# Thirty-one expert blocks in a new order, a block's transposes inside the next block's products, the first gather in one piece

## The chip, the cores and the metric

The program runs on one core of a Trainium2 chip. The metric is the device time of one execution in microseconds (us). One execution was also taken by the hardware profiler, and all rows below come from it.

## What is computed

Two transformer blocks follow each other on 256 tokens of width 1024, in float32. The change lies in the mixture of experts (MoE) at the end of the first one: 64 experts, each token goes to 8 of them, and the results are added up by token.

```python
def moe_ffn(h, router_w, router_bias, w_gate, w_up, w_down, sh_gate, sh_up, sh_down):
    ...
    scores = jax.nn.sigmoid((hf @ router_w).astype(jnp.float32))
    ...
    _, e_idx = lax.top_k(jnp.where(expert_mask, biased, -jnp.inf), TOP_K)
    gate = jnp.take_along_axis(scores, e_idx, axis=1)
    gate = gate / jnp.sum(gate, axis=-1, keepdims=True) * ROUTED_SCALE
    ...
    def expert_block(args):
        xb, e = args
        return (jax.nn.silu(xb @ w_gate[e]) * (xb @ w_up[e])) @ w_down[e]
    yb = lax.map(expert_block, (xin, block_expert)).reshape(n_rows, d)
    routed = jax.ops.segment_sum(yb * row_gate[:, None], row_tok, num_segments=T + 1)[:T]
    shared = (jax.nn.silu(hf @ sh_gate) * (hf @ sh_up)) @ sh_down
    return (routed + shared).reshape(b, s, d)
```

Each of an expert's three matrices (w_gate, w_up, w_down; 1024 x 256 or 256 x 1024 float32) is 1 MiB, so all experts together are 192 MiB.

## The kernel before

**Blocks.** Once the router's result is known, the experts are ranked by their number of tokens; the two experts 0 and 1 are fixed at ranks 0 and 1, so that their weights can be loaded ahead. `CAPS` gives each rank a capacity in slots: ranks 0 and 1 have 128, ranks 2 and 3 have 256, ranks 4 to 11 have 128, the next 20 have 64, the last 32 have 32. A block is 128 slots: one expert of 128, half of one of 256, two experts of 64 or four of 32. That makes 32 blocks. `PH` holds a phase for each kind, and the blocks of each kind are spread evenly by it; the order is, by number of experts in a block, 1 1 4 1 1 2 4 1 1 2 4 1 2 1 4 2 1 2 4 1 2 4 1 2 4 1 2 1 4 2 1 2 (the pairs "1 1" with one weight set are the halves of ranks 2 and 3).

**A block's work on TensorE**, which runs in the order of the program text (as SyncE does; the other engines' order is set by a scheduler after the start of the stage):

- every fourth block `onehots` (VectorE, tile `D`) compares slots with token positions, `gather` (L1400, tile `xgp`, evacuated to `xg` by ScalarE) fetches the tokens of four blocks by 32 products of 512 columns, and `slots` (L1384, tile `sp`) makes the scatter matrices;
- `gate_up(b)` (L1442, tile `gu`): eight products for w_gate and eight for w_up of each expert. Blocks of two or four experts put their experts side by side into 64 or 32 columns of the array (`tile_position`); each float32 product is two TensorE instructions, so a block of one expert shows as x32, of two as x64, of four as x128;
- ScalarE's Silu and one VectorE operation make `act`;
- `down(b)`: two transposes of `act` (L1459, tile `at`), ScalarE's copy to `aT` (L1461), products with w_down (L1468, tile `dn`), then `y` in two float32r parts by VectorE, ScalarE and GpSimd (L1476 to L1478; VectorE in place of GpSimd in the last two blocks);
- `scatter(b)` (L1490, tile `sc`) for two blocks at a time, 16 products of 512 columns added to the tokens.

The loop calls `gate_up(b + 1)`, then, for every second b, `scatter` of the two finished blocks, then `down(b)`.

**Weights.** `Stream` lists the loads in the order in which the blocks need them; SyncE issues one as soon as a buffer of 1 MiB is free (14 of them: 5 `wraw`, 6 `mraw`, 3 of `whi` and `wlo` together), and goes by a list in strict order. Which experts are to be loaded is known only when the router is done (`eid`).

**The start of the stage.** `shared_up(m)` (L1078, tile `sh`) issues m of the 32 products of the shared expert to fill TensorE while VectorE works out the routing. The first gather takes only the first block's 128 columns; the other 384 follow after the first block's products.

Of the kernel before, what the change touches and what calls it, by code (L numbers as in the profile page):

```python
# [18 lines left out]
F32 = mybir.dt.float32  # L19
# [7 lines left out]
T = 256  # L27
ALPHA = 2.0 ** 0.25
TOPG = 4
SHARED = int('16')  # L30
PH = {1: 0.7, 2: 0.95, 4: 0.1}
FIXED = int('2')
CAPS = ((128, FIXED), (256, 2), (128, 10 - FIXED), (64, 20), (32, 32))


class Stream:
# [86 lines left out]
def build(ctx, tc, I, out, dbg=None, stop=None):  # L123
# [640 lines left out]
    for i in range(4):  # L764
        p = plin("pyb")
# [317 lines left out]
    blocks = []  # L1083
    r0 = 0
    for c, n in CAPS:
        r = r0
        while r < r0 + n:
            if c >= 128:
                for q in range(c // 128):
                    blocks.append([(r, 128 * q, 128)])  # L1090
                r += 1
            else:
                blocks.append([(r + m, 0, c) for m in range(128 // c)])
                r += 128 // c
        r0 += n
    NBL = len(blocks)

    kinds = {}
    for b in blocks[FIXED:]:
        k = kinds.setdefault(len(b), [])  # L1100
        if b[0][1]:
            k[-1].append(b)
        else:
            k.append([b])
    place = [((i + PH[n]) / len(k), u) for n, k in kinds.items() for i, u in enumerate(k)]
    blocks = blocks[:FIXED] + [b for _, u in sorted(place, key=lambda q: q[0]) for b in u]
    def onehots(gi, Dt, lo=0, hi=4):

        bl = blocks[4 * gi:4 * gi + hi]
# [59 lines left out]
    neg_exp(1, pr1)  # L1169
    A.activation(x2h[:, 1, :], xnm[:, 1, :], AF.Copy)  # L1170
    psh += [pacc("sh0"), plin("sh1")]
    shared_up(16)
    scores(1)

    gsc = rtemp("gsc", (128, 2, 8))
# [116 lines left out]
    io256 = moe.tile([128, 256], F32, name="io256")  # L1292
    G.iota(io256, pattern=[[1, 256]], base=1, channel_multiplier=0, allow_small_or_imprecise_dtypes=True)
    D0 = moe.tile([128, 2, 512], F32R, tag="D", name="D0", bufs=1)
    onehots(0, D0, 0, 1)
    low(1)
    gsum = rtemp("gsum", (128, 2, 1))
    V.tensor_reduce(gsum, gt_, axis=AX.X, op=OP.add)
    V.reciprocal(gsum, gsum)
    for t in range(2):  # L1300
        V.tensor_scalar(gt_[:, t, :], gt_[:, t, :], gsum[:, t, :], 2.5, op0=OP.mult, op1=OP.mult)
    onehots(0, D0, 1, 4)
    dump("sel", sel.bitcast(F32), lambda d: d.rearrange("(t p) e -> p t e", p=128))
    dump("gate", gt_, lambda d: d.rearrange("(t p) e -> p t e", p=128))

# [70 lines left out]
    def slots(gi, Dt):  # L1376

        bl = blocks[4 * gi:4 * gi + 4]
        St = moe.tile([128, 4, 256], F32R, tag="S", name=f"S{gi}", bufs=2)
        gc = moe.tile([128, 4], F32, tag="gc", name=f"gc{gi}", bufs=2)  # L1380
        for b in range(4):
            p = paux(f"sp{gi}_{b}")
            for t in range(2):
                PE.matmul(p[:, 128 * t:128 * t + 256], Dt[:, t, 128 * b:128 * b + 128], idg[:, t, :],  # L1384
                          start=(t == 0), stop=(t == 1), skip_group_check=True)
            A.activation(St[:, b, :].rearrange("p (t n) -> p t n", t=2),
                         p[:, :384].rearrange("p (t n) -> p t n", t=3)[:, 0::2, :], AF.Copy)
            for k, (r, _, c) in enumerate(bl[b]):
                s_ = slice(c * k, c * k + c)
                V.tensor_scalar(gc[s_, b:b + 1], p[s_, 128 + r:129 + r], p[s_, 192 + r:193 + r], None, op0=OP.add)  # L1390
        return St, gc
# [23 lines left out]
    def pairs(b):  # L1415
        return [list(enumerate(blocks[b]))]

    def gate_up(b):
        gi, bb = divmod(b, 4)
        if bb == 0:  # L1420
            if gi:
                Dt = moe.tile([128, 2, 512], F32R, tag="D", name=f"D{gi}", bufs=1)
                onehots(gi, Dt)
            else:
                Dt = D0
            xg = tail.tile([128, 8, 512], F32, tag="big2", name=f"xg{gi}")
            grp[gi] = [None, None, xg, Dt]
            if gi:
                gather(gi, Dt, xg)
                grp[gi][:2] = slots(gi, Dt)  # L1430
            else:
                gather(gi, Dt, xg, 0, 128)
                gate_slots()
                shared_end()
        xg = grp[gi][2]
        p = plin(f"gu{b}")
        for ex in pairs(b):
            for w, off in (("g", 0), ("u", 256)):
                wts = [wtile(r, w) for _, (r, _, _) in ex]
                for j in range(8):  # L1440
                    for (k, (r, b0, c)), wt in zip(ex, wts):
                        PE.matmul(p[c * k:c * k + c, off:off + 256], xg[:, j, 128 * bb + c * k:128 * bb + c * k + c],  # L1442
                                  wt[j], start=(j == 0), stop=(j == 7), tile_position=(0, c * k))
                for _, (r, _, _) in ex:
                    wdone(r, w)
        if b == 0:
            grp[gi][:2] = slots(gi, grp[gi][3])
            gather(gi, grp[gi][3], xg, 128, 512)
        act = moe.tile([128, 256], F32, tag="act", name=f"act{b}", bufs=2)
        A.activation(act, p[:, 0:256], AF.Silu)  # L1450
        last_act[0] = V.scalar_tensor_tensor(act, act, grp[gi][1][:, bb:bb + 1], p[:, 256:512], op0=OP.mult, op1=OP.mult)  # L1451
        return act

    last_sub = [None]

    def down(b, act):
        p = paux(f"at{b}")
        for j in range(2):
            PE.transpose(p[:, 128 * j:128 * j + 128], act[:, j::2], ident)  # L1459
        aT = moe.tile([128, 2, 128], F32, tag="aT", name=f"aT{b}", bufs=2)  # L1460
        A.activation(aT, p[:, :256].rearrange("p (j s) -> p j s", j=2), AF.Copy)  # L1461
        pd = [paux(f"dn{b}_{h}") for h in range(2)]
        for ex in pairs(b):
            wts = [wtile(r, "d") for _, (r, _, _) in ex]
# [9 lines left out]
        for h in range(2):  # L1474
            hs_ = slice(512 * h, 512 * h + 512)
            V.tensor_mul(yf[:, h, :], pd[h], g2[:, hs_])  # L1476
            A.activation(y[:, 0, hs_], yf[:, h, :], AF.Copy)  # L1477
            last_sub[0] = (V if b >= NBL - 2 else G).tensor_sub(y[:, 1, hs_], yf[:, h, :], y[:, 0, hs_].bitcast(F32))  # L1478
        return y

    def scatter(b, ys):

        St, bb = grp[b // 4][0], b % 4
        for t in range(2):
            for h in range(2):
                p = plin(f"sc{b}_{t}{h}")
                q = 0
                for m in range(2):
                    for k in range(2):
                        PE.matmul(p, St[:, bb + m, 128 * t:128 * t + 128], ys[m][:, k, 512 * h:512 * h + 512],  # L1490
                                  start=(q == 0), stop=(q == 3))
                        q += 1
                o = acc[:, t, 512 * h:512 * h + 512]
                if b == NBL - 2:
                    V.scalar_tensor_tensor(o, p, 1.0, o, op0=OP.mult, op1=OP.add, accum_out=sums[:, 0, t, h:h + 1])
                elif b == 0:
                    V.scalar_tensor_tensor(o, o, ALPHA, p, op0=OP.mult, op1=OP.add)
                else:
                    V.tensor_add(o, o, p)
# [42 lines left out]
    overflow()  # L1542
    ws.ahead = 1
    for b in range(NBL):
        nxt = gate_up(b + 1) if b + 1 < NBL else None
        if len(ys) == 2:
            scatter(b - 2, ys)
            ys = []
        ys.append(down(b, act))
        act = nxt  # L1550
        if b == 2:
            prepare_loads()
# [5 lines left out]
    ln2 = ws.take_raw(ln2_req)  # L1558
    ln2g, ln2b = ln2[:, 0:D], ln2[:, D:2 * D]
    rg = moe.tile([128, 2, D], F32, tag="mraw", name="rg", bufs=6)  # L1560
    scatter(NBL - 2, ys)

    flag = nc.values_load(ovi[0:1, 0:1], min_val=0, max_val=64 * T)
    with tc.If(flag > 0):
# [413 lines left out]
```

## Time and profile before

| | |
|---|---|
| median of 3 runs | 1369.22 us (1369.01 to 1376.6) |
| the profiled execution | 1372.89 us, its span 1371.1 us |
| the MoE stage, first expert product to end of the last scatter | 511.6 to 1022.4 us of the span |
| TensorE (PE) busy | 1284.9 us, 94% of the span |
| VectorE, ScalarE, GpSimd busy | 60%, 41%, 13% |
| HBM read | 377.59 MB |

A span's time is counted from its own start. The profile's page cuts the span into 40 slices of 34.3 us; counted from 0, slices 15 to 29 hold the MoE stage.

### The profile page before, as it was taken

The numbers are of one execution on the slowest core, as the hardware profiler recorded it, in microseconds if no ns is written. First come the engines' busy times: TensorE is split into PE (matmuls) and PEld (weight loads), VectorE is DVE, ScalarE is ACT, GpSimd is POOL, SyncE is SP. The second block draws the span as 40 slices with busy tenths as digits, with TensorE's granted clock in tenths as the row PEclk, the third lists the DMA queues.
The fourth block names the chain that finished last, engine by engine and source line by source line (L and its number), as shares of the span: only waits on it lengthen the run. The fifth ranks groups of instructions, "written<-read, shape, count | busy, mean of one in ns | idle before, by whom it ended". The sixth has DMA issues, their size and how long they took to land.

```text
span 1371.1 us, 22687 instructions
## 1 busy us (share of the span) xinstructions
PE 1284.9 (94%) x9042; PEld 1051.5 (77%) x9042; DVE 818.2 (60%) x1331; ACT 567.7 (41%) x862; POOL 178.3 (13%) x169
## 2 busy tenths in 40 slices
PE   3989999999999899999999999999988999899997
PEld 1989988789899687757675756667648887899985
DVE  2999998978898731222223232221255577788995
ACT  1675644445654422313131313223126655666642
POOL 1011243411100100221111111211110000000000
PEclk9999999999999979999999999999998999999999
DMA  9967776669788476989899999999995334455550
GB/s 340 324 220 261 247 237 224 214 217 314 239 306 285 173 298 257 383 308 368 337 419 401 417 411 419 418 418 418 418 335 174 128 118 154 137 182 183 176 184 32
DMA packets 148977, 380.21 MB, mean 277 GB/s; under 512 B 7839, under 2 KB 97285, under 8 KB 129028
## 3 DMA queue, kind: packets, MB, share of 16 engines
q1 hardware_dynamic: 145856, 373.20, 74.3%
q0 software_dynamic: 2240, 5.34, 1.3%
q8 instruction: 72, 1.18, 0.3%
q10 hardware_dynamic: 772, 0.19, 0.1%
q14 instruction: 37, 0.30, 0.1%
HBM read 377.59 MB, written 1.10 MB: 276 GB/s over the span
## 4 chain that ended last, share of the span: by engine, by line
PE 61%; DVE 4%; issue 3%; ACT 2%; DMA 1%; POOL 0%; POOLq 0%; DVEq 0%; ACTq 0%
PE gu L1442 16%; PE dn L1468 8%; PE xgp L1400 5%; PE sc L1490 4%; PE pgt L555 2%; PE pgt L556 2%; PE pgt L557 2%; PE pvl L557 2%; PE pvl L555 2%; PE pvl L556 2%; PE pf L907 1%; PE pf L909 1%; PE pf L905 1%; DVE wlo L199 1%; PE sh L1078 1%
## 5 line engine op out<-in xcount | busy, mean ns | idle before, releaser
L195 ACT ACTIVATE whi<-wraw 128x1024 fp32r<-128x1024 f32 x216 | 228.1, 1058 | 240.9 <-PE pf L909 30.8
L199 DVE TENSOR_TENSOR wlo<-wraw,whi 128x1024 fp32r<-128x1024 f32 x216 | 271.1, 1257 | 64.2 <-ACT whi L195 62.9
L1442 PE MATMUL gu<-mraw,xg 128*32 128x256 f32 (+2 forms) x944 | 147.0, 380 | 0.3 <-DMA mraw<-in_w_up_dram 0.3
L1478 POOL TENSOR_TENSOR y<-yf,y 128x512 fp32r<-128x512 f32 x60 | 76.8, 1280 | 441.3 <-ACT y L1477 441.3
L1451 DVE SCALAR_TENSOR_TENSOR act<-act,gc,gu 128x256 f32<-128x256 f32 x32 | 15.4, 480 | 190.3 <-ACT act L1450 190.2
L1442 PEld LDWEIGHTS gu<-mraw,xg 128*32 128x32 f32 (+2 forms) x944 | 96.5, 136 | 29.9 <-issue 7.8
L1476 DVE TENSOR_TENSOR yf<-dn,g 128x512 f32<-128x512 f32 x64 | 44.2, 691 | 93.3 <-PE dn L1468 93.3
L1450 ACT ACTIVATE act<-gu 128x256 f32<-128x256 f32 x32 | 12.3, 384 | 199.2 <-PE gu L1442 199.2
L1442 PE MATMUL gu<-wraw,xg 128*32 128x256 f32 (+2 forms) x672 | 93.6, 380 | 0.0
L1477 ACT ACTIVATE y<-yf 128x512 fp32r<-128x512 f32 x64 | 40.3, 630 | 123.4 <-DVE yf L1476 123.4
L557 PE MATMUL pl<-hh,wlo 128*128 128x256 f32 x256 | 74.4, 292 | 4.2 <-DVE wlo L199 4.2
L1442 PEld LDWEIGHTS gu<-wraw,xg 128*32 128x32 f32 (+2 forms) x672 | 58.3, 130 | 23.9 <-DVE yf L1476 2.5
L1468 PE MATMUL dn<-wraw,aT 128*32 128x512 f32 (+2 forms) x232 | 69.5, 598 | 6.9 <-ACT aT L1461 6.9
L1468 PE MATMUL dn<-mraw,aT 128*32 128x512 f32 (+2 forms) x208 | 69.4, 598 | 6.2 <-ACT aT L1461 6.2
L555 PE MATMUL pl<-hh,whi 128*128 128x256 f32 x256 | 73.9, 289 | 0.0
L556 PE MATMUL pl<-hl,whi 128*128 128x256 f32 x256 | 73.7, 288 | 0.0
L431 DVE SCALAR_TENSOR_TENSOR adac<-wraw,csil,adac 128x1024 f32<-128x1024 f32 x49 | 67.1, 1370 | 5.9 <-DMA wraw<-in_w_ada_dram 5.3
L1490 PE MATMUL sc<-y,S 128*128 128x512 f32 x256 | 65.2, 405 | 0.1
L1400 PE MATMUL xgp<-D,x2h 128*128 128x512 f32 (+2 forms) x144 | 61.1, 424 | 0.9 <-DVE D L1118 0.9
L1402 ACT ACTIVATE xg<-xgp,mvp 128x512 f32<-128x512 f32 (+2 forms) x72 | 52.5, 730 | 19.1 <-PE xgp L1400 14.6
L1400 PE MATMUL xgp<-D,x2l 128*128 128x512 f32 (+2 forms) x144 | 58.8, 408 | 0.3 <-DVE x2l L1070 0.3
L1490 PEld LDWEIGHTS sc<-y,S 128*128 128x128 f32 x256 | 47.3, 188 | 14.9 <-issue 3.1
(575 smaller groups left out, 3565.2 us busy)
## 6 DMA issues: line engine op xcount, KB each, us to landing
wraw<-in_w_in_dram SPq DMA_DIRECT2D x56, 1024.0 KB, 6.2
wraw<-in_w_ada_dram SPq DMA_DIRECT2D x47, 1024.0 KB, 7.2
wraw<-in_w_up_dram SPq DMA_DIRECT2D x39, 1024.0 KB, 9.5
wraw<-in_w_down_dram SPq DMA_DIRECT2D x38, 1024.0 KB, 4.9
mraw<-in_w_up_dram SPq DMA_DIRECT2D x30, 1024.0 KB, 13.0
mraw<-in_w_gate_dram SPq DMA_DIRECT2D x27, 1024.0 KB, 16.1
mraw<-in_w_down_dram SPq DMA_DIRECT2D x26, 1024.0 KB, 14.9
wraw<-in_w_gate_dram SPq DMA_DIRECT2D x25, 1024.0 KB, 12.5
```

Of the source, the lines that this page charges most:

```text
L195: A.activation(hi, v, AF.Copy)
L199: V.tensor_sub(lo, v, hi.bitcast(F32))
L431: V.scalar_tensor_tensor(acc, wv[:, k, s_], c, acc, op0=OP.mult, op1=OP.add)
L555: PE.matmul(o, wh[:, k, :], xh[:, k0 + k, :], start=(k == 0), stop=False)
L556: PE.matmul(o, wh[:, k, :], xl[:, k0 + k, :], start=False, stop=False)
L557: PE.matmul(o, wl[:, k, :], xh[:, k0 + k, :], start=False, stop=(k == 7))
L1400: PE.matmul(p[:, :c1 - c0], src[:, t, j::8], Dt[:, t, c0:c1], start=(q == 0), stop=(q == 3))
L1402: A.activation(xg[:, j, c0:c1], p[:, :c1 - c0], AF.Identity, scale=mvp[:, 1, j:j + 1], bias=mvp[:, 0, j:j + 1])
L1442: PE.matmul(p[c * k:c * k + c, off:off + 256], xg[:, j, 128 * bb + c * k:128 * bb + c * k + c], wt[j], start=(j == 0), stop=(j == 7), tile ...
L1468: last_dn[0] = PE.matmul(pd[h][c * k:c * k + c, :], aT[:, j, c * k:c * k + c], wt[j][:, 512 * h:512 * h + 512], start=(j == 0), stop=(j == ...
L1478: last_sub[0] = (V if b >= NBL - 2 else G).tensor_sub(y[:, 1, hs_], yf[:, h, :], y[:, 0, hs_].bitcast(F32))
L1490: PE.matmul(p, St[:, bb + m, 128 * t:128 * t + 128], ys[m][:, k, 512 * h:512 * h + 512], start=(q == 0), stop=(q == 3))
```

## The change

The two experts at ranks 2 and 3 get 192 slots instead of 256: two blocks of 128, and a third in which the last 64 slots of both share the array. That makes 31 blocks. The order of all but the first two is written out in a table, `ORDER` (`w` stands for these three blocks in a row): 1 1 4 2 1 2 2 4 1 2 2 2 1 4 1 1 2 4 1 2 1 1 4 4 1 1 2 4 2 2 4. `down` is split: its transposes and the copy become `turn(b)`, which is called inside `gate_up(b + 1)`, between the w_gate and the w_up products. The first gather takes all 512 columns at once. `shared_up` issues 10 products instead of 16 before the routing's counts. The shared expert's last product moves from block 16 to block 8. With an odd number of blocks the last scatter holds one block (`LAST`), and VectorE makes `y`'s second part only for that one.

```diff
-SHARED = int('16')
-PH = {1: 0.7, 2: 0.95, 4: 0.1}
+SHARED = int('8')
 FIXED = int('2')
-CAPS = ((128, FIXED), (256, 2), (128, 10 - FIXED), (64, 20), (32, 32))
+CAPS = ((128, FIXED), (192, 2), (128, 10 - FIXED), (64, 20), (32, 32))
...
-            if c >= 128:
-                for q in range(c // 128):
-                    blocks.append([(r, 128 * q, 128)])
+            if c == 192:
+                blocks += [[(r, 0, 128)], [(r + 1, 0, 128)], [(r, 128, 64), (r + 1, 128, 64)]]
+                r += 2
+            elif c == 128:
+                blocks.append([(r, 0, 128)])
                 r += 1
...
+    LAST = (NBL - 1) // 2 * 2
+    aTs = {}
...
+    ORDER = "4212241222141124121144w4224"
...
-    shared_up(16)
+    shared_up(10)
...
-    onehots(0, D0, 0, 1)
+    onehots(0, D0)
     low(1)
...
-    onehots(0, D0, 1, 4)
...
-    def gate_up(b):
+    def gate_up(b, between=None):
...
-                gather(gi, Dt, xg, 0, 128)
+                gather(gi, Dt, xg)
                 gate_slots()
                 shared_end()
...
+                if w == "g" and between:
+                    between()
         if b == 0:
             grp[gi][:2] = slots(gi, grp[gi][3])
-            gather(gi, grp[gi][3], xg, 128, 512)
...
-    def down(b, act):
+    def turn(b, act):
         p = paux(f"at{b}")
         for j in range(2):
             PE.transpose(p[:, 128 * j:128 * j + 128], act[:, j::2], ident)
         aT = moe.tile([128, 2, 128], F32, tag="aT", name=f"aT{b}", bufs=2)
         A.activation(aT, p[:, :256].rearrange("p (j s) -> p j s", j=2), AF.Copy)
+        aTs[b] = aT
+
+    def down(b):
+        aT = aTs.pop(b)
...
-            last_sub[0] = (V if b >= NBL - 2 else G).tensor_sub(y[:, 1, hs_], yf[:, h, :], y[:, 0, hs_].bitcast(F32))
+            last_sub[0] = (V if b >= LAST else G).tensor_sub(y[:, 1, hs_], yf[:, h, :], y[:, 0, hs_].bitcast(F32))
...
     for b in range(NBL):
-        nxt = gate_up(b + 1) if b + 1 < NBL else None
+        if b + 1 < NBL:
+            nxt = gate_up(b + 1, lambda: turn(b, act))
+        else:
+            turn(b, act)
         if len(ys) == 2:
             scatter(b - 2, ys)
             ys = []
-        ys.append(down(b, act))
+        ys.append(down(b))
```

TensorE around the routing, before: the shared expert's first 16 products, the counts (`pcnt`) and positions, two more shared products, then the first gather with 128 columns.

```order
L1078 MATMUL sh_5158<-h2f,mraw_5029 128x256 x16
L1204 MATMUL pcnt<-room_5042,ones_r 64x64 x2
L1206 MATMUL pcnt<-ones_r,room_5042 64x2 x2
L1211 MATMUL psel<-idg,room_5042 64x128 x2
L1212 MATMUL ppos<-room_5042 64x128
L1213 MATMUL ppos<-ones_r,room_5042 64x128
L1214 MATMUL ppos<-room_5042 64x128
L1078 MATMUL sh_5159<-h2f,mraw_5031 128x256 x2
L1225 MATMUL peid<-rt_Pm,room_5042 2x64
L1286 MATMUL pk<-rt_Pm,room_5042 128x64 x2
L1400 MATMUL xgp_0_0_5319<-D_5288,x2h 128x128
```

The same place after the change:

```order
L1077 MATMUL sh_5158<-h2f,mraw_5029 128x256 x10
L1205 MATMUL pcnt<-room_5042,ones_r 64x64 x2
L1207 MATMUL pcnt<-ones_r,room_5042 64x2 x2
L1212 MATMUL psel<-idg,room_5042 64x128 x2
L1213 MATMUL ppos<-room_5042 64x128
L1214 MATMUL ppos<-ones_r,room_5042 64x128
L1215 MATMUL ppos<-room_5042 64x128
L1077 MATMUL sh_5158<-h2f,mraw_5029 128x256 x2
L1226 MATMUL peid<-rt_Pm,room_5042 2x64
L1287 MATMUL pk<-rt_Pm,room_5042 128x64 x2
L1400 MATMUL xgp_0_0_5311<-D_5282,x2h 128x512
```

Six of the shared products have gone from the front, and the gather's products are 512 columns wide; the six stand now behind the gather, ahead of the first `gu`.

TensorE in block 1 and block 0 (`gu` of block 1, `at` and `dn` of block 0), before:

```order
L1442 MATMUL gu_5516<-mraw_5033,xg_5318 128x256 x8
L1442 MATMUL gu_5516<-wraw_5035,xg_5318 128x256 x8
L1459 MATMUL at_5540<-ident,act_5507 128x128 x2
L1468 MATMUL dn_0_5545<-wraw_5037,aT_5543 128x512 x2
L1468 MATMUL dn_1_5546<-wraw_5037,aT_5543 128x512 x2
```

After:

```order
L1442 MATMUL gu_5476<-mraw_5033,xg_5310 128x256 x8
L1460 MATMUL at_5487<-ident,act_5467 128x128 x2
L1442 MATMUL gu_5476<-wraw_5035,xg_5310 128x256 x8
L1473 MATMUL dn_0_5505<-wraw_5037,aT_5490 128x512 x2
L1473 MATMUL dn_1_5506<-wraw_5037,aT_5490 128x512 x2
```

The transposes stand between the w_gate and the w_up products, and `dn` follows the last `gu` with nothing between them.

ScalarE over the same blocks and the next one, before:

```order
L1450 ACTIVATE act_5537<-gu_5516 128x256
L1461 ACTIVATE aT_5543<-at_5540 128x256
L1477 ACTIVATE y_5553<-yf_5554 128x512 x2
L1450 ACTIVATE act_5684<-gu_5561 128x256
L1461 ACTIVATE aT_5690<-at_5687 128x256
L1477 ACTIVATE y_5709<-yf_5710 128x512 x2
```

After:

```order
L1462 ACTIVATE aT_5490<-at_5487 128x256
L1451 ACTIVATE act_5502<-gu_5476 128x256
L1482 ACTIVATE y_5513<-yf_5514 128x512 x2
L1462 ACTIVATE aT_5578<-at_5575 128x256
L1451 ACTIVATE act_5631<-gu_5521 128x256
L1482 ACTIVATE y_5651<-yf_5652 128x512 x2
```

The copy to `aT` has moved ahead of the Silu of the following block (`act`).

## Rows read from the trace of the kernel before

**Rows 1.** The page's 40 slices: busy tenths of the DMA engines.

```profile
DMA  9967776669788476989899999999995334455550
```

**Rows 2.** Windows: PE, PEld, DVE, ACT, POOL busy (instructions), clock, DMA share, GB/s.

```profile
525.00:550.00 25.00, 24.01 (x191) 15.84 (x191) 4.79 (x14) 4.98 (x11) 2.57 (x2) 1.00 0.61 221
...
650.00:675.00 25.00, 23.93 (x226) 13.79 (x224) 5.55 (x9) 3.22 (x7) 3.97 (x4) 1.00 0.79 296
...
875.00:900.00 25.00, 24.47 (x176) 18.55 (x176) 7.91 (x23) 9.18 (x16) 2.77 (x3) 1.00 1.01 419
```

**Rows 3.** Chain that ended last, in the MoE stage: start, us, engine, tile, line.

```profile
519.59 7.78 PE xgp L1400 x32
...
707.60 0.38 ACT act L1450
...
708.50 3.70 PE dn L1468 x8
712.20 6.91 PE gu L1442 x32
719.11 3.74 PE sc L1490 x16
722.85 0.24 PE at L1459 x2
723.18 0.39 ACT aT L1461
723.61 3.65 PE dn L1468 x16
...
739.46 7.06 PE gu L1442 x64
746.51 3.94 PE sc L1490 x16
...
754.85 8.15 PE xgp L1400 x32
763.00 0.95 PE sp L1384 x8
```

**Rows 4.** Timeline around the routing: start, us, engine, line, operation, what it waited for.

```profile
481.75 9.43 PE L1078 MATMUL sh<-h2f,mraw 128*128 128x256 f32 x32
...
487.28 0.23 DVE L1194 TENSOR_SCALAR room<-room 128x128 fp32r<-128x128 f32 x1
...
490.83 0.44 PE L1204 MATMUL pcnt<-room,ones_r 128*64 128x64 f32 x2
...
493.66 0.49 DVE L1118 TENSOR_TENSOR D<-io,rt_posr 128x128 fp32r<-128x128 f32 x2
...
495.34 0.46 PE L1400 MATMUL xgp<-D,x2l 128*128 128x128 f32 x1 [0.34 <-DVE x2l L1070]
...
502.37 0.63 PE L1318 MATMUL psel<-ident,rt_gate 128*64 128x128 f32 x2
...
507.14 4.59 PE L1078 MATMUL sh<-h2f,mraw 128*128 128x256 f32 x20
...
511.57 7.07 PE L1442 MATMUL gu<-mraw,xg 128*128 128x256 f32 x32
```

**Rows 5.** Windows of 5 us around the routing, TensorE alone: busy, granted clock, DMA share, GB/s.

```profile
500.00:505.00 5.00, 5.00 (x19) 0.50 0.95 335
```

**Rows 6.** First expert load after the routing, from the timeline.

```profile
494.07 1.53 SPq L332 DMA_DIRECT2D wraw<-in_w_gate_dram  x2
```

**Rows 7.** Waits of SyncE's DMA queue, 480 to 1060 us: total us, times, longest.

```profile
SPq L332 <- PE gu L1442: 69.6, 24, 12.0
```

**Rows 8.** Who TensorE's gate and up products waited for, by line: us, times.

```profile
  DMA mraw<-in_w_up_dram: 1.1, 2
```

**Rows 9.** GpSimd's share of y, from the timeline.

```profile
972.51 1.28 POOL L1478 TENSOR_TENSOR y<-yf,y 128x512 fp32r<-128x512 f32 x1 [0.37 <-ACT y L1477]
```

**Rows 10.** The stage's last down product, from the timeline.

```profile
1015.18 3.65 PE L1468 MATMUL dn<-mraw,aT 128*64 128x512 f32 x16
```

More of the change, by code (lines that the diff above doesn't have):

```diff
@@ L1096, in build @@
     NBL = len(blocks)
[L1098 to L1106, printed above, removed]
+    LAST = (NBL - 1) // 2 * 2
+    aTs = {}
+    ORDER = "4212241222141124121144w4224"
+    kinds = {"w": [blocks[FIXED:FIXED + 3]]}
+    for b in blocks[FIXED + 3:]:
+        kinds.setdefault(str(len(b)), []).append([b])
+    assert all(ORDER.count(k) == len(v) for k, v in kinds.items())
+    blocks = blocks[:FIXED] + [b for k in ORDER for b in kinds[k].pop(0)]
     def onehots(gi, Dt, lo=0, hi=4):
@@ L1380, in slots @@
         gc = moe.tile([128, 4], F32, tag="gc", name=f"gc{gi}", bufs=2)
-        for b in range(4):
+        for b in range(len(bl)):
             p = paux(f"sp{gi}_{b}")
@@ L1428, in gate_up @@
             if gi:
-                gather(gi, Dt, xg)
+                gather(gi, Dt, xg, 0, 128 * len(blocks[b:b + 4]))
                 grp[gi][:2] = slots(gi, Dt)
             else:
-                gather(gi, Dt, xg, 0, 128)
+                gather(gi, Dt, xg)
                 gate_slots()
@@ L1487, in scatter @@
                 q = 0
-                for m in range(2):
+                for m, y in enumerate(ys):
                     for k in range(2):
-                        PE.matmul(p, St[:, bb + m, 128 * t:128 * t + 128], ys[m][:, k, 512 * h:512 * h + 512],
-                                  start=(q == 0), stop=(q == 3))
+                        PE.matmul(p, St[:, bb + m, 128 * t:128 * t + 128], y[:, k, 512 * h:512 * h + 512],
+                                  start=(q == 0), stop=(q == 2 * len(ys) - 1))
                         q += 1
                 o = acc[:, t, 512 * h:512 * h + 512]
-                if b == NBL - 2:
+                if b == LAST:
                     V.scalar_tensor_tensor(o, p, 1.0, o, op0=OP.mult, op1=OP.add, accum_out=sums[:, 0, t, h:h + 1])
@@ L1560, in build @@
     rg = moe.tile([128, 2, D], F32, tag="mraw", name="rg", bufs=6)
-    scatter(NBL - 2, ys)
+    scatter(LAST, ys)
     flag = nc.values_load(ovi[0:1, 0:1], min_val=0, max_val=64 * T)
```

## Prediction

> **What bounds the kernel now.** I read the page's slices first [rows 1]: slices 15 to 29 are the MoE stage, and from slice 20 on the DMA engines stand at 9 of 10. TensorE is busy 24 of 25 us in each window of the same stage [rows 2]. So two things can set the end of this stage, and a change that shortens one may only uncover the other. The windows sharpen this: at 525 us the DMA engines are busy 0.61 of the time, at 650 us 0.79, and at 875 us 1.01 with 419 GB/s, about the most that any window shows. The waits say who waits for whom: SyncE's queue stood 69.6 us waiting for gate and up products to give buffers back [rows 7], while those products waited for weights only 1.1 us in all [rows 8]. TensorE's own order of work is therefore the bound, with the weights close behind. The chain of waits shows what that order consists of [rows 3]: gate and up 6.91 (one expert) or 7.06 us (two), down 3.65 to 3.70, a scatter of two blocks 3.74 or 3.94, a gather 8.15 and its slots 0.95 for four blocks. Between them stands one stretch in each block in which TensorE does little: 0.24 us of transposes, then a wait for ScalarE's copy, 0.76 us from 722.85 to 723.61; where no scatter precedes, it is about 0.92 us (707.6 to 708.5), because the copy first queues behind the Silu.
>
> **The start.** The first 32 `sh` instructions (16 products) take 9.43 us, and the counts wait for them: the selection is ready at 487.28 + 0.23 = 487.51, the counts start at 490.83 [rows 4]. Ten products take 10/16 x 9.43 = 5.9 us and end at 487.6, so the routing chain moves up 3.2 us, and the first load of a routed expert with it, from 494.07 [rows 6] to 490.9. Six compares for `D` instead of two then stand ahead of the second half of x2l on VectorE; two take 0.49 us, so about 1.1 us more. The gather's fourth product waits for x2l and moves from 495.34 to 495.34 - 3.2 + 1.1 = 493.2. Twenty-nine products of 512 columns follow. At the full clock one takes 8.15/32 = 0.255 us [rows 3]. Around 500 us the granted clock is 0.50 of full, 1.2 instead of 2.4 GHz [rows 5], after the short products and gaps of the routing; no row here shows 512 columns at that level, and twice the price is the upper bound: 7.4 to 14.8 us, and I take 9.8, the clock rising on the way as it did before. The gather ends at 503.0, where it ended at 502.4. The six moved shared products (12 instructions at 4.59/20 = 0.23) add 2.8; the eight shared instructions between may run faster by 1. So the first `gu` moves from 511.57 to 513.9, and the second gather, 7.78 us [rows 3], is gone: 2.3 - 7.8 = **-5.5** (-8 with the clock full throughout, -0.5 with half clock throughout).
>
> **One block less.** Gate and up 7.0, down 3.7, a quarter of 0.95, and the last gather has three blocks, 8.15 - 7.78 = 0.37: **-11.3**. The number of scatters stays the same.
>
> **The transposes.** Thirty-two waits of 0.76 or 0.92, about half each, but part of the longer ones is not the copy: I take 0.79, so -25.4. What comes back: 31 x 0.24 = 7.4 for the transposes themselves. `act` is made before the preceding `dn` runs, so they find it ready, and the copy (0.39) hides under 3.5 us of w_up products. Their place costs something, though. After a block of two, whose products use half-width columns, a scatter takes 3.94 instead of 3.74 [rows 3]: going from split to full width costs 0.20. Nineteen of the new blocks are split, and each now switches to full width and back in the middle: 19 x 0.25 = 4.8, and about 1 more where `dn` follows directly on split products. Sum **-12.2** (-18 if switching is free).
>
> The Trainium skill, "TensorEngine Tiling (Array Packing)", section Tiling Modes, says that changing the tiling mode drains the engine, not only changing the tile. That speaks against just this place, and it gives no price; the 0.20 us agrees with a drain in kind. A drain of the length of a product at each switch would be the second rival below.
>
> **The end.** Block 29's y was covered by the following block's products before its scatter. Now only block 30's transposes stand between, and the last GpSimd part, 1.28 us [rows 9], comes late: **+1.3** (0 to 2.6). The last scatter has half its products (3.74/2 at most), but waits for the same chain on VectorE: **-0.3** (-1.9 to 0).
>
> **Do the weights keep up?** 62 experts x 3 + 1 = 187 loads of 1 MiB; at 419 GB/s one takes 2.50 us, in all 468 us. On the path: five buffers are free at the first issue and are filled by about 506; the next come free when the shared products end (513.9), so the queue starts again at about 516 with 182 loads left, 455 us. Without any idle time they end at 971; TensorE's last `dn` ended at 1018.8 [rows 10] and ends, by the sums above, at 992, of which that product itself is 3.7. Some 17 us are spare in total, but they are not evenly spread. The order puts many loads early, and the queue can run ahead by 14 buffers at most, so it idles wherever blocks of one follow each other. The tight point is the two blocks of four in a row, 22 and 23: by block 22's `dn`, 141 of the 187 loads are needed. With some 10 us of idle time up to there the 141st lands at 516 + 136 x 2.50 + 10 = 866. TensorE gets there at 522 (block 1) + 23 gu x 7.0 + 22 dn x 3.7 + 11 scatters x 3.85 + 5 gathers x 9.1 + the shared product 6.9 + 23 transposes x 0.4 = 868. From there to the last load are 46 x 2.50 = 115 us, 981, against a last `dn` that is to start at 988. Both points are met with a few us or less to spare: **+1** for waits (0 to 6).
>
> Sum: -5.5 - 11.3 - 12.2 + 1.3 - 0.3 + 1 = **-27.0**. Behind the stage nothing is bound by DMA (slices 30 to 39 stand at 3 to 5 of 10 [rows 1]), so the loss is not caught up later. The profiled execution took 1372.89 us with a span of 1371.1; it becomes 1345.9. The runs' median lies 3.7 below it, at 1369.2: **1342 us**.
>
> **The rivals.**
>
> *The DMA queue idles as early as before.* Between 525 and 675 us the six windows' shares leave some 22 us idle (0.61 and 0.79 are the ends [rows 2]). If the buffers come back as slowly in the new order, the last weight lands at 971 + 22 + the later idle 10 = 1003 and its `dn` ends at 1007: 1369 - 12 = 1357. Against it: a block of two or four brings twice or four times the bytes in the same TensorE time, and these now come early.
>
> *Each switch drains a product.* If each of the 38 new switches costs the time of one product alone, 0.46 us [rows 4], instead of 0.25 for two, 17.5 us replace 4.8: 1355. For it: the trace has no transposes between two split products. Against it: 0.20, and 0.24 for `at` itself.
>
> *Capacity.* Ranks 2 and 3 have 192 slots instead of 256. If an expert had more tokens than its capacity, the kernel would run its overflow branch, which loads all 64 experts once more, one after the other, in the open: 64 x 3 x 2.50 = 480 us at least, so 1822 or more, slower. It decides at 193 tokens. Worked out from the reference's inputs, the largest count beside the fixed experts is 157, and the third is 90.
>
> *The order does nothing.* If neither transposes nor gather moved, one block less alone gives 1369 - 11 = 1358; but the instruction order shows that both moved, so this gets no chance.
>
> **How the numbers follow.** Forecast 1342, with its own range 1335 to 1349 from the bounds of start, switches and waits: chance 0.74. DMA idling 1357: 0.10. Drains 1355: 0.08. Better than 1335, the clock full and the switches free: 0.05. Capacity or another mishap that makes it slower: 0.03. The range 1334 to 1355 takes in the forecast and the drains. About 1% (13.7 us) is what a measurement of this kernel can tell from no change: the forecast and the better case lie beyond it, the drains and the idling queue at its edge, and I count half of these two as faster. Faster 0.88, same 0.09, slower 0.03.
>
> **What the profile would show.** Right: no wait of `dn` for `aT`; gate and up with the transposes about 7.3 (one expert) to 7.6 us; the counts near 487.7; the first `gu` near 514; the DMA share near 1 from 550 on; the last `dn` near 992. Wrong: `gu` or `dn` waiting for a load for more than 6 us in all, above all at blocks 22 and 23 or in the last four; more than 0.5 us added at a split switch; a gather of over 12 us at half clock.

## The result and the profile after

The changed kernel takes **1338.64 us** (median of 4 runs, 1337.4 to 1340.41), the kernel before, run beside it, 1372.91 us (4 runs, 1369.01 to 1381.96): ratio **0.9755, 95% interval 0.9727 to 0.9782**. The profiled execution took 1340.41 us with a span of 1338.5 us, where before it was 1371.1.

Four points of both timelines place the 32.6 us of span: the first shared product, the first `gu` of block 1, the end of the last `dn` and the end of the span.

| | before | after | |
|---|---|---|---|
| up to the first shared product | 481.8 | 481.5 | -0.2 |
| start: from there to block 1 | 45.7 | 38.3 | -7.4 |
| blocks: from there to the end of the last `dn` | 491.4 | 466.3 | -25.1 |
| the rest | 352.3 | 352.4 | +0.1 |

The page's slices, busy tenths of the DMA engines, to be held against [rows 1]. The stage's first slices (15 to 19), a six and eights among nines there, are an eight and nines now:

```profile
DMA  9977766759889288999999999999995334455450
```

Windows of 25 us, columns as in [rows 2]:

```profile
525.00:550.00 25.00, 25.00 (x225) 14.05 (x224) 3.73 (x6) 4.43 (x9) 5.12 (x4) 1.00 0.91 349
550.00:575.00 25.00, 25.00 (x131) 19.12 (x132) 8.47 (x21) 9.24 (x17) 7.29 (x11) 1.00 1.02 412
575.00:600.00 25.00, 25.00 (x170) 14.83 (x168) 6.15 (x10) 4.05 (x8) 5.11 (x4) 1.00 1.02 417
600.00:625.00 25.00, 25.00 (x205) 16.13 (x202) 6.33 (x10) 7.88 (x12) 5.14 (x4) 1.00 1.02 417
625.00:650.00 25.00, 25.00 (x164) 17.11 (x164) 8.12 (x21) 5.44 (x12) 2.55 (x2) 1.00 1.01 419
650.00:675.00 25.00, 25.00 (x145) 12.84 (x145) 8.80 (x14) 3.63 (x7) 5.09 (x4) 1.00 1.02 419
...
850.00:875.00 25.00, 23.83 (x205) 14.33 (x204) 5.99 (x9) 6.35 (x11) 5.14 (x4) 1.00 1.02 419
875.00:900.00 25.00, 25.00 (x135) 19.77 (x135) 6.79 (x19) 6.98 (x14) 2.54 (x2) 1.00 1.01 419
```

TensorE is busy 25.00 of 25 us where it was 24; from 550 to 975 us the DMA engines stand at 0.93 to 1.02 at the same time. Both resources are now nearly full together. Between 525 and 975 us one window alone falls short for TensorE, 850 to 875, and the timeline names the wait:

```profile
866.12 3.62 PE L1473 MATMUL dn<-wraw,aT 128*32 128x512 f32 x26 [1.17 <-DMA wraw<-in_w_down_dram]
```

That is `dn` of block 22, the point that the prediction called tight. The chain of waits over two blocks of one and two experts, columns as in [rows 3]:

```profile
566.12 3.46 PE gu L1442 x16
569.58 0.23 PE at L1460 x2
569.81 3.46 PE gu L1442 x16
573.27 3.58 PE dn L1473 x16
576.85 3.45 PE gu L1442 x32
580.31 0.44 PE at L1460 x2
580.75 3.60 PE gu L1442 x32
584.35 3.93 PE sc L1495 x16
588.28 3.43 PE dn L1473 x8
```

No ScalarE row stands between the products any more. The transposes cost 0.23 us inside a block of one expert and 0.44 inside a split block, and `dn` of a block of one takes 3.43 where it took 3.70 [rows 3]. The start, in the chain:

```profile
490.84 1.57 DVE D L1119 x6
492.41 1.15 DVE x2l L1069
493.55 0.04 issue
493.60 8.56 PE xgp L1400 x29
502.16 0.22 PE psel L1318 x2
502.38 1.74 PE sh L1077 x8
```

The same 29 products of the first gather, in the chain of the kernel before, where they had 128 columns and a second piece (7.78 us, [rows 3]) followed:

```profile
495.34 7.23 PE xgp L1400 x29
```

With 512 columns they take 8.56 us, in part at the lower clock. So a product of 128 columns took nearly as long, and the two pieces cost nearly two whole gathers.

And the last scatter of a pair, which waits for GpSimd's part of block 29's y:

```profile
979.56 2.37 PE L1495 MATMUL sc<-y,S 128*128 128x512 f32 x9 [0.48 <-POOL y L1483]
```

### The profile page after: what moved, and what is told of

Same layout as the page of the kernel before. It is cut to its first block, busy times and chain, and to the rows that moved or that the text cites. A ratio compares the mean times of both kernels' runs of the same rounds, so it can differ in the third digit from the quotient of the medians.

```text
span 1338.5 us, 22545 instructions
## 1 busy us (share of the span) xinstructions
PE 1268.3 (95%) x8998; PEld 1029.2 (77%) x8998; DVE 813.3 (61%) x1306; ACT 562.1 (42%) x849; POOL 178.9 (13%) x169
## 4 chain that ended last, share of the span: by engine, by line
PE 62%; DVE 5%; DMA 4%; issue 1%; ACT 1%; POOL 0%; SPq 0%; DVEq 0%; POOLq 0%; ACTq 0%
PE gu L1442 16%; PE dn L1473 8%; PE xgp L1400 5%; PE sc L1495 4%; PE pgt L554 2%; PE pgt L555 2%; PE pgt L556 2%; PE pvl L554 2%; PE pvl L556 2%; PE pvl L555 2%; PE pf L906 1%; PE pf L908 1%; PE pf L904 1%; DVE wlo L198 1%; DMA wraw<-in_w_down_dram 1%
## 5 line engine op out<-in xcount | busy, mean ns | idle before, releaser
L1442 PE MATMUL gu<-mraw,xg 128*32 128x256 f32 (+2 forms) x976 | 135.1, 381 | 0.0
L1442 PEld LDWEIGHTS gu<-mraw,xg 128*32 128x32 f32 (+2 forms) x976 | 86.7, 135 | 22.7 <-issue 5.3
L1442 PE MATMUL gu<-wraw,xg 128*32 128x256 f32 (+2 forms) x704 | 98.7, 381 | 0.0
L1402 ACT ACTIVATE xg<-xgp,mvp 128x512 f32<-128x512 f32 (+1 forms) x64 | 48.8, 764 | 18.7 <-PE xgp L1400 18.5
L1400 PE MATMUL xgp<-D,x2h 128*128 128x512 f32 (+1 forms) x128 | 55.0, 429 | 1.4 <-DVE D L1119 1.4
L1473 PE MATMUL dn<-mraw,aT 128*32 128x512 f32 (+2 forms) x200 | 55.2, 596 | 0.0
L556 PEld LDWEIGHTS pl<-hh,wlo 128*128 128x128 f32 x256 | 49.6, 194 | 6.2 <-DVE wlo L198 5.8
L1400 PE MATMUL xgp<-D,x2l 128*128 128x512 f32 (+1 forms) x128 | 53.0, 414 | 0.4 <-DVE x2l L1069 0.4
```

What stands on the lines that cost most here:

```text
L556: PE.matmul(o, wl[:, k, :], xh[:, k0 + k, :], start=False, stop=(k == 7))
L1400: PE.matmul(p[:, :c1 - c0], src[:, t, j::8], Dt[:, t, c0:c1], start=(q == 0), stop=(q == 3))
L1402: A.activation(xg[:, j, c0:c1], p[:, :c1 - c0], AF.Identity, scale=mvp[:, 1, j:j + 1], bias=mvp[:, 0, j:j + 1])
L1473: last_dn[0] = PE.matmul(pd[h][c * k:c * k + c, :], aT[:, j, c * k:c * k + c], wt[j][:, 512 * h:512 * h + 512], start=(j == 0), stop=(j == ...
```

## The experiments

Each kernel ran beside the kernel before on its chip (medians 1371.5 to 1371.7 us). Times outside the changed stage differ by some us from run to run, so each is judged by the two stretches of the table above too, read off its own timeline: *start* (before 45.7, after 38.3) and *blocks* (before 491.4, after 466.3). Where the instructions of a stretch are the same, these readings repeat well: the start is 37.9 to 38.7 in the eight kernels with the new start, the blocks 466.3 to 467.0 in three kernels and 480.6 and 480.7 in two. One part of the change was not undone by itself, the shared expert's last product in block 8 instead of 16: it takes 7.0 us in both kernels, and what its place brings counts here with the order. A dense block is one of four experts, with twelve loads, a sparse one a block of one expert. A "loss" in a block is the time from a tile's first instruction to that of the next tile beyond the usual one of its kind.

**The transposes alone, in the kernel before,** with `down` split into `turn` and `down` as in the change.

```diff
...
-        nxt = gate_up(b + 1) if b + 1 < NBL else None
+            nxt = gate_up(b + 1, lambda: turn(b, act))
...
```

> The kernel before with one part alone: the transposes inside the next block's products. Theory (TensorE's own order is the bound, and each wait removed from it counts): 31 waits of about 0.8 us go, 31 x 0.23 us and 19 x 0.20 us for the switches come back, and a product after no wait is 0.1 to 0.3 us shorter, so about 16 us by TensorE; but the last weights landed only some 12 us ahead of their product, so 2 to 6 us come back as waits for loads in the last third: 10 to 15 us faster than before, 1354 to 1359. Rival (the order of the blocks made the gain, the transposes hide nothing that mattered): within 3 us of before, with the waits for the copy turned into waits for loads.

1366.84 us, ratio 0.9963 (0.9951 to 0.9976); start 45.4, blocks 483.3. Of 16 us only 8.1 arrive in the blocks, and 4.7 in the whole time, which lies 8 us above the range expected. The rest is in waits for weights that the kernel before hardly had, in the second half of the stage; two of them by line:

```profile
L1476 PE MATMUL dn<-mraw,aT 128*32 128x512 f32 x96 | 26.4, 595 | 1.2 <-DMA mraw<-in_w_down_dram 1.2
L1442 PE MATMUL gu<-wraw,xg 128*64 128x256 f32 x160 | 26.3, 382 | 0.8 <-DMA wraw<-in_w_gate_dram 0.8
```

The idle times are short, but each wait also stretches the products around it: nine places lose 9.6 us together. With them the 8.1 come to 17.7, near the 16 that the theory gave to TensorE; it was wrong on what the old order lets through.

**The change with the old sequence of kinds.**

```diff
-    ORDER = "4212241222141124121144w4224"
+    ORDER = "4w2424121421241241241214212"
```

> The changed kernel with its 31 blocks in the old succession (4 w 2 4 2 4 1 2 1 4 2 1 2 4 1 2 4 1 2 4 1 2 1 4 2 1 2). Theory (TensorE is now so short that the weights are level with it, and the new order is what keeps the DMA queue busy early): gate, up and down products wait for loads 15 to 25 us in all, most of it after two thirds of the blocks, so 1354 to 1363. Rival (the order changes nothing, TensorE's sum is all): 1337 to 1342, waits for loads under 3 us.

1364.06 us, ratio 0.9948 (0.9927 to 0.997); start 37.9, blocks 492.6, 26.3 us more than in the changed kernel: as much as the change gained in the blocks. The order is not quite the old one, though. Both large experts stand at the first one's place, and at the second one's 2 4 2 4 follow each other with no sparse block between: these 31 blocks take 9.3 us longer than the 32 of the run above (483.3). So 26.3 us is the price of this order, not of every order but the new one. Where it goes, in windows:

```profile
575.00:600.00 25.00, 25.00 (x170) 14.81 (x170) 6.35 (x10) 3.42 (x7) 4.86 (x4) 1.00 0.66 250
...
850.00:875.00 25.00, 20.26 (x145) 9.30 (x138) 2.88 (x5) 3.28 (x6) 5.08 (x4) 0.86 1.01 417
...
925.00:950.00 25.00, 22.38 (x181) 12.55 (x180) 2.39 (x4) 3.19 (x7) 4.74 (x4) 0.86 1.02 418
```

Full buffers leave the DMA engines idle at 575 (0.66, with one wait of SyncE's queue of 19.3 us for `gu`); at 850 and 925 dense blocks wait for loads, and the granted clock drops to 0.86 with the idle TensorE. This is what the prediction's first rival described, in an order that the change does not have.

**The change without the move of the transposes.**

```diff
-            nxt = gate_up(b + 1, lambda: turn(b, act))
+            nxt = gate_up(b + 1)
...
+        turn(b, act)
         ys.append(down(b))
```

> The changed kernel with the transposes back behind the scatter, straight ahead of the down products. Theory: 12 to 18 us slower than the change, 1351 to 1357, TensorE idle before nearly every down product and no wait for loads left. Rival (weights are the bound, waits of TensorE are filled anyway): less than 4 us slower.

1354.4 us, ratio 0.9869 (0.9847 to 0.9892); blocks 480.7, so the move is worth 14.4 us there. The wait is back, in its chain:

```profile
586.86 3.93 PE sc L1495 x16
590.79 0.24 PE at L1460 x2
...
591.12 0.39 ACT aT L1462
591.51 0.04 issue
591.56 3.70 PE dn L1473 x8
```

The move brings 8.1 us with the old order and its 32 blocks and 14.4 with the new order and 31: its worth hangs on the sequence around it.

**The change with the old start.**

```diff
-    shared_up(10)
+    shared_up(16)
...
-                gather(gi, Dt, xg)
+                gather(gi, Dt, xg, 0, 128)
...
+            gather(gi, grp[gi][3], xg, 128, 512)
```

> The changed kernel with the old start: 16 shared products ahead of the counts, the first gather in two pieces. Theory: the second block's products start at about 527.5 again instead of 519.7, and all behind moves with them: 7 to 9 us slower, 1346 to 1348. Rival (the weights set the end; their first load moves only 2.8 us): 3 to 4 us slower, the rest made up by shorter waits for loads.

1354.16 us (1346.39 to 1355.66), ratio 0.9856 (0.982 to 0.9892). The whole is 6 us above the range expected, and some 15 above the changed kernel; the stretches are start 45.6 (+7.3) and blocks 467.0 (+0.7). The rest of the profiled run's excess lies ahead of the stage (first shared product at 484.4 instead of 481.5) and behind it (+2.9), where both kernels have the same instructions. The profile doesn't show what causes it, so only the stretches bear out the theory; the last section has what goes with it.

**Both undone: 31 blocks in the new order alone.** The two edits above together.

> The changed kernel with two of its parts undone at once: transposes right ahead of the down products, and 16 products ahead of the counts with a gather in two pieces. What is left is 31 blocks in the new order. If the parts add up (15.8 us for the transposes, 7.6 for the start), 1338.6 + 23.4 = 1362 us; stage from the second block to the last dn as without the transposes' move, 480 to 482 us. Rival (the parts need each other: a slower TensorE lets the loads run ahead, and full buffers then stop the queue, as in the kernel before): 1366 to 1371 us, 485 us or more, with waits for weights of 5 us or more in the stage.

1364.79 us, ratio 0.9924 (0.9893 to 0.9955); start 45.2, blocks 480.6. The whole lies between theory (1362) and rival (1366), so the stretches decide, and in them the theory holds: against the kernel before, 491.4 - 480.6 = **10.8 us** for one block less with the order, then 480.6 - 466.3 = **14.3** for the transposes, and 7 for the start. The rival (full buffers) is out: only `dn` of block 22 takes longer than its kind for a load, by 1.1 us. Block and order are not told apart here. But the gate and up products of the kernel before waited only 1.1 us for weights [rows 8], so a better order alone had little to win there, and the runs with 32 blocks below price a block by itself.

**16 shared products ahead, gather in one piece.**

```diff
-    shared_up(10)
+    shared_up(16)
```

> The changed kernel with 16 products of the shared expert ahead of the scores instead of 10, the gather in one piece as changed. Theory (the one-piece gather brought nearly all of the 7.6 us of the start, and the earlier counts only what the six products cost there less what they cost behind the gather at full clock): from the first shared product to the second block 39.5 to 40.5 us against 38.3, 1 to 2 us more in all, 1340 to 1341. Rival 1 (the counts are waited for, so 6 x 0.44 us come on top whole): 41 us. Rival 2 (products ahead of the routing keep the clock up, and the gather then runs at the full level from its start): 37 us, 1 us less.

1341.21 us, ratio 0.9784 (0.9767 to 0.9801); start 39.5, blocks 466.5. Of the start's 7.4 us the one-piece gather brings 6.2 and the earlier counts 1.2, as the theory had it; 39.5 lies 0.8 above the highest of the eight kernels with the new start.

**Transposes ahead of the scatter where one follows.**

```diff
+        cover = len(ys) == 2 or b + 1 == NBL
         if b + 1 < NBL:
-            nxt = gate_up(b + 1, lambda: turn(b, act))
-        else:
+            nxt = gate_up(b + 1, None if cover else lambda: turn(b, act))
+        if cover:
             turn(b, act)
```

> The changed kernel, with the two transposes of a block put ahead of the scatter wherever a scatter follows (14 of 31 blocks), and inside the next block's products as before elsewhere. Theory (each switch between split and whole tiles costs 0.20 us, and a scatter of 3.7 to 3.9 us covers the copy as well as products do): 11 of the 14 blocks have a split successor, so 11 x 0.20 = 2.2 us less, some 1336.5 us against 1338.6. Rival 1 (the copy aT stands in ScalarE's queue behind the block's Silu, which needs the product that ends just ahead of the scatter, so dn waits again): 14 x up to 0.5, no change to 7 us more, 1339 to 1346 us. Rival 2 (the switch is only moved, to the scatter): within 0.5 us of 1338.6.

1339.21 us, ratio 0.9743 (0.9713 to 0.9773); blocks 463.7, so 2.6 us less there, as 11 switches of 0.20 give (2.2). In the whole time it can't be told from the changed kernel. Its chain at the place of the chain shown above:

```profile
578.61 6.91 PE gu L1442 x64
585.52 0.44 PE at L1460 x2
585.96 3.73 PE sc L1495 x16
589.69 3.43 PE dn L1473 x8
```

The switch from split to full columns is paid once, by the transposes (0.44), and the scatter behind them takes 3.73 instead of 3.93.

**32 blocks, all else as changed.**

```diff
-CAPS = ((128, FIXED), (192, 2), (128, 10 - FIXED), (64, 20), (32, 32))
+CAPS = ((128, FIXED), (256, 2), (128, 10 - FIXED), (64, 20), (32, 32))
...
-                blocks += [[(r, 0, 128)], [(r + 1, 0, 128)], [(r, 128, 64), (r + 1, 128, 64)]]
+                blocks += [[(r, 0, 128)], [(r, 128, 128)]]
...
```

> The changed kernel with 32 blocks: the two large experts get 256 places each again (four blocks of one expert where the change has three), all else as changed. Theory (TensorE is never idle in the stage, so a block costs its products, gather, scatter and transposes): a block of one expert is 6.92 (gu) + 3.6 (dn) + 0.23 + a quarter of a gather of 8 us (the last group has four blocks again) + half a scatter (0.5 x (3.92 x 2 - 3.9)) = 12 to 13 us more, less nothing: 1350 to 1352 us. Rival (the weights set the pace, so a block that loads no weights is partly free): 1339 to 1346 us.

1363.32 us, ratio 0.9935 (0.991 to 0.9961); blocks 489.0, 22.7 more, 10 above the theory. Windows of 5 us show why:

```profile
930.00:935.00 5.00, 5.00 (x29) 4.82 (x32) 0.00 (x0) 4.07 (x7) 0.00 (x0) 1.00 0.00 0
...
980.00:985.00 5.00, 1.24 (x4) 0.28 (x4) 0.00 (x0) 0.00 (x0) 0.00 (x0) 1.00 1.01 421
```

Four sparse blocks in a row (two experts, six loads) leave every buffer full: SyncE issues no load from 919 to 938 us (one wait of 19.1 us), and from 925 to 935 the DMA engines move next to nothing. The four blocks behind them (4 2 2 4) want 36 loads, and at 980 TensorE is busy 1.24 of 5 us. Whether that is the block's price or its place, the next run tells.

**32 blocks in an order of their own.**

```diff
-    ORDER = "4212241222141124121144w4224"
+    ORDER = "42124211244112222211244w414"
```

> The 32 blocks of the earlier run again, in an order made for them (the four blocks of the two large experts one place from the fourth-last block's group, sparse and dense blocks spread so that, by the trace's 2.5 us for a load and the thirteen buffers, no product waits). Theory (that run paid 12 to 13 us for the block and the other 10 us for weights that its order asked for too late): the stage from the second block's first product to the last dn takes 475 to 478 us, against 489.0 in the earlier run and 466.3 in the changed kernel, and the whole 1348 to 1351 us. Rival (a block of one expert itself costs 20 us or more, as the range of orders tried so far can't exclude): 487 to 490 us, 1360 to 1364.

1351.87 us, ratio 0.9852 (0.9834 to 0.9869); blocks 477.4. A block costs 11.1 us, and the other 11.6 were the order's. The rival (20 us for the block itself) is out.

**24 loads left out.** Blocks of four use their first expert's w_down for all four, so that the output lacks the other experts' own.

```diff
+    def lead(r, w):
+        return r - r % 4 if w == "d" and r >= 32 else r
...
-            for r in ex:
+            for r in [lead(r, w) for r in ex]:
...
```

> The changed kernel, with the down weights of the first expert of each block of four used for all four, so that 24 of the stage's 187 weight loads are left out (the output lacks those experts' own down weights; the products are as many as before). Theory (TensorE bounds the stage, and weights are waited for 1.2 us in one place): 1 to 2 us less, 1336.5 to 1338 us. Rival (the transfers still set the pace, and products queue behind them in ways that the idle time doesn't show): 24 x 1 MiB / 420 GB/s = 60 us of transfer less would give 5 to 20 us, 1319 to 1334 us.

1342.84 us, ratio 0.9765 (0.9725 to 0.9804): no faster in the whole, and 5 us above the range expected. Blocks 463.5, 2.8 us less, though the DMA engines' share falls below 0.95 in seven of eighteen windows (0.63 at 750, 0.51 at 900). So beyond the waits at block 22 (2.2 us) these transfers cost the changed kernel next to nothing: TensorE bounds it. The profiled run (1345.3) reached the stage only at 488.5 instead of 481.5, ahead of anything that the edit touches.

**Four loads more.**

```diff
+        if b + 1 == 22:
+            order += [("x", i) for i in range(4)]
...
```

> The changed kernel with four more weight loads of 1 MiB (a copy of expert 0's gate weights, never used) queued ahead of block 22's. Theory (the ledger of loads is level with TensorE at block 22, where the trace shows 1.2 us of wait for dn): 4 x 2.5 us = 10 us of transfer come on top, of which the later blocks can't take anything back: 8 to 10 us more, 1346 to 1349 us. Rival (loads have slack of their own, as the idle DMA queues after 975 us suggest): 0 to 3 us more, 1339 to 1342 us.

1347.62 us, ratio 0.9806 (0.9766 to 0.9845); blocks 474.2, 7.9 more for 10 us of transfer. The extra loads also keep four buffers, and this run doesn't tell the two apart; either way there is next to no slack at block 22:

```profile
862.08 0.62 PE L1456 MATMUL gu<-wraw,xg 128*32 128x256 f32 x2 [1.88 <-DMA wraw<-in_w_up_dram]
864.59 6.14 PE L1456 MATMUL gu<-wraw,xg 128*32 128x256 f32 x58 [1.90 <-DMA wraw<-in_w_up_dram]
```

**Four small steps more.** The kernel with the transposes ahead of the scatter, and:

```diff
-    ORDER = "4212241222141124121144w4224"
+    ORDER = "4221242221412114141142w4224"
...
+    low(1)
     cnt = rtemp("cnt", (64, 66))
...
-    low(1)
...
-            last_sub[0] = (V if b >= LAST else G).tensor_sub(...)
+            last_sub[0] = (V if b >= LAST - 1 else G).tensor_sub(...)
...
```

> The changed kernel with four small steps more: the transposes ahead of the scatter where one follows (measured, 2.6 us of stage), the low half of the second 128 tokens made while VectorE waits for the counts instead of behind them (1.15 us off the path to the gather), the next-to-last block's low half of y on VectorE instead of GpSimd (1.1 us of the last scatter), and an order of blocks in which dn of block 22 needn't wait (1.2 us). Theory: all four add up, 6 us less: from the first shared product to the second block 37.2 us, from there to the last dn 461.5 us, 1332 to 1334 us in all. Rival (the gather starts 1.1 us sooner but at the half clock level for as much longer, and the order moves the wait elsewhere): 2 to 3 us less, 1335.5 to 1337.

1345.28 us, ratio 0.9806 (0.9782 to 0.983); start 38.0, blocks 468.5. Slower than the changed kernel, so my theory fell: none of the three new steps brought its saving. First, the gather no longer waits for x2l, but VectorE starts `D` 0.2 us later (9.5 us after the first shared product instead of 9.3), and more of the gather runs at the lower clock. The loss of clock is the same (0.66 in one window here, 0.80 and 0.86 in two windows of the changed kernel), but here it falls on the gather alone: eight of its products start 0.43 us apart (500.20 to 503.61), in the changed kernel five (494.21 to 496.35).

```profile
495.00:500.00 5.00, 3.53 (x22) 1.00 0.16 29
500.00:505.00 5.00, 5.00 (x16) 0.66 0.95 390
...
498.78 9.87 PE xgp L1400 x32
```

So 0.3 us of start is left of 1.1, no more than kernels with the same start differ by. Second, the last scatter of a pair waits for y as long as in the changed kernel (0.46 us, there 0.48), now for VectorE instead of GpSimd:

```profile
986.33 2.36 PE L1495 MATMUL sc<-y,S 128*128 128x512 f32 x9 [0.46 <-DVE y L1483]
```

Third, the order moves the waits instead of removing them: `gu` of a block of four at 800 us waits 1.9 us, the last `dn` 1.5; with what they stretch, its blocks lose some 7 us where the changed order loses 2.2. No run here beats the changed kernel by its whole time; the transposes ahead of the scatter are the only step that shortens its stage with the same work done.

## Why the prediction was right

The time came out in the range, 3.4 us below the forecast of 1342, but the saving was larger than forecast: 32.6 us of span instead of 27.0. The forecast was counted from 1369.2, and the kernel before took 1372.91 beside the changed one, so the two medians lie 34.3 apart. That the forecast time came closer than the forecast saving is chance. The mechanism held; two terms were too small.

- **The bound** (TensorE's own order, weights close behind) holds: 25.00 of 25 us busy, 24 loads less bring 2.8 us, four more cost 7.9.
- **The start**: forecast -5.5, measured -7.4. The counts began at 488.0 (forecast 487.6) and the gather's products behind x2l at 493.60 (493.2), but the gather ended at 502.0 (503.0): 8.56 us for 29 products where 9.8 was taken, since the granted clock was back at its full level early (0.80, 0.86 and 1.00 in the windows from 490 to 505). The prediction took it to rise during the gather "as it did before"; in the kernel before it stood at 0.50 from 500 to 505 [rows 5], to the gather's end and beyond. What follows the gather grew by 0.4 us only, not by 1.8, since the shared products there ran at the full clock too (1.74 us for eight in the chain above, 3.41 in the chain before). First `gu` at 511.6 instead of 513.9.
- **One block less**: forecast -11.3, to which its transposes and wait (0.8) come, which the forecast counts in the next term. The new order alone brings 10.8, with block 22's wait (1.1) and the end's wait for y (5.09 us for that scatter instead of 3.8, so 1.2) already in it; without them 13.1, beside 12.1. A block added to the changed kernel costs 11.1. Right within 1 us.
- **The transposes**: the mechanism was right, the term too small. Forecast -12.2 for 32 blocks; measured 14.3 net for 31, with block 22's further 1.1 us of waiting in it. The forecast took 0.79 us for a wait from the chain [rows 3] (32 x 0.79 is 25.3, put down as 25.4). By the starts in the timeline of the new order alone, the stretch from the transposes to `dn` takes 29.8 us in 31 blocks, 0.96 each: the product behind a wait is itself longer in the chain, 3.70 instead of 3.43, and the forecast gave that to `dn`. With the move 11.0 us are left, of which 31 x 0.23 are the transposes and 19 x 0.20 the switches, and `gu` takes 213.0 us from block 1 on instead of 209.9, since both halves of a split block now take 3.60 (half of 7.06 before). So the cost of their new place was forecast well, 13.2, measured 11.0 + 3.1 = 14.1; the step that was mis-sized is the 0.79.
- **The switch** does cost: 0.44 against 0.23, the same 0.20 that a scatter behind a split block showed, and eleven switches less brought 2.6 us. The rule of the Trainium skill, "TensorEngine Tiling (Array Packing)", Tiling Modes, that a change of mode drains the engine, agrees in kind; as a rival at 0.46 for each switch it is out.
- **The end**: +1.3 forecast for y, 1.1 measured. The last `dn` ends at 986.1 (forecast 992): the start and the transposes make the difference.
- **Waits for weights**: forecast +1 with the tight point at block 22; 1.2 us of idle time just there, 2.2 with the products that it stretches. The rival of the idling queue (1357) did not happen in this order: in the six windows from 525 to 675 us the DMA engines' shares leave some 2 us idle, where they left 22 before. But the prediction has the order down as no more than a condition to check, with 6 us at stake. In the run with the old sequence of kinds the blocks take 492.6 us, no less than the 491.4 before the change: with that order the block left out and the transposes together gain nothing.

Start, new order and transposes are stretches of one table, split at the 480.6 of the new order alone, so that their sum (7.4 + 10.8 + 14.3 = 32.5 of 32.6) had to come out and proves nothing by itself.

## What to carry to other kernels

When two resources are nearly level, price a saving on one together with the sequence that feeds it: the same transposes were worth 8.1 us with the old order of blocks and 14.3 with the new, and an order planned to take the wait from block 22 lost some 5 us. Read a wait's cost from start to start of the work around it rather than from its idle time, which missed 0.17 us per wait for the copy here, and about half of the wait for weights at block 22. A step that needs another tiling of the array belongs where a switch is paid anyway.

## What the runs showed of the hardware beyond that

- The granted clock differs a little from run to run, and the time with it. Over 97 runs of these kernels, each against the mean of its own kernel on its chip, a mean granted clock lower by 0.001 goes with 0.9 us more of span (correlation -0.82). The changed kernel's runs had 0.979 to 0.982; those of the run with fewer loads 0.970 to 0.978, of which the lowest has a span of 1343.5 us and the highest 1336.3. Brought to the same clock in this way, that kernel, the one with the old start and the one with the transposes ahead of the scatter come out 4 us below, 8 above and 3 below the changed kernel, as their stretches say. What makes the clock differ, and whether it is the cause of the longer time or goes along with it, no run here shows.
- In the changed kernel products of 512 columns start 0.43 us apart (494.21, 494.64, 495.07) while the granted clock is 0.50, the lower of its levels (1.2 GHz), and 0.245 apart at 1.00 (2.4 GHz): less than twice, so the half clock costs a gather less than its ratio. In the kernel before, products of 128 columns start 0.24 apart at either level (496.12, 496.36, 496.60 at the full one, 501.41, 501.65, 501.89 at the lower one) and those of 384 columns 0.24 apart at the full one. At the full clock, then, fewer columns than 512 bring next to nothing here, which is why a gather in two pieces costs so much. The kernel before, at the full level and at the lower one:

```profile
496.36 0.40 PE L1400 MATMUL xgp<-D,x2l 128*128 128x128 f32 x1
496.60 0.45 PE L1400 MATMUL xgp<-D,x2h 128*128 128x128 f32 x1
...
501.41 0.44 PE L1400 MATMUL xgp<-D,x2h 128*128 128x128 f32 x1
501.65 0.44 PE L1400 MATMUL xgp<-D,x2l 128*128 128x128 f32 x1
```

- From 550 to 975 us the DMA engines moved 362 to 422 GB/s with TensorE busy 25 of 25 us in all windows but one. Transfers and products didn't slow each other there: a whole gather took 7.83 us in the run with 32 blocks, while the DMA engines stood still (first row below), and 7.81 in the changed kernel (second row) with 423 to 426 GB/s beside it (windows under it).

```profile
926.17 7.83 PE xgp L1400 x32
...
807.20 7.81 PE xgp L1400 x32
...
805.00:810.00 5.00, 5.00 (x19) 3.93 (x18) 1.38 (x2) 2.63 (x4) 2.59 (x2) 1.00 1.01 423
810.00:815.00 5.00, 5.00 (x23) 4.95 (x23) 0.00 (x0) 3.90 (x5) 0.00 (x0) 1.00 1.02 426
```
